# Single-column Newton steps with per-partition scalars, and weight slabs subtracted in four pieces, in a two-block transformer kernel

## The chip, the cores and the metric

The kernel runs on one core of one Trainium2 chip. The metric is the device time of one execution in microseconds (us), as the median of several runs. A core has a matrix engine (PE, with its weight loads as PEld), a vector engine (DVE, VectorE), an activation engine (ACT, ScalarE), a GpSimd engine (POOL) and a queue engine that only starts transfers (SP). Each runs its own instructions in program order and waits on semaphores for the others.

## The reference

The reference is two transformer blocks of two layers each, on 512 tokens of width 1024 in float32. The first block has a gated delta rule layer and a dilated attention layer, the second has two layers with neighbourhood attention, spatial gating and grouped-query attention, modulated by a conditioning vector. A SwiGLU feed-forward net follows each of the four. What matters for the change is that each sublayer begins or ends with a normalisation of every token, and that each holds large products with weight matrices:

```python
def _rmsnorm(x, w):
    xf = x.astype(jnp.float32)
    y = xf * lax.rsqrt(jnp.mean(xf * xf, axis=-1, keepdims=True) + RMS_EPS)
    return (y * w.astype(jnp.float32)).astype(x.dtype)

def layer_norm(x):
    xf = x.astype(jnp.float32)
    mu = jnp.mean(xf, -1, keepdims=True)
    var = jnp.mean(jnp.square(xf - mu), -1, keepdims=True)
    return ((xf - mu) * lax.rsqrt(var + LN_EPS)).astype(x.dtype)

def swiglu(h, w_in, w_out):
    a, b = h @ w_in[:, :D_FF], h @ w_in[:, D_FF:]
    return (jax.nn.silu(a) * b) @ w_out

# second block, layer l
mod = split_cols((sc @ w_mod[l] + b_mod[l])[:, None, :], (D_MODEL,) * N_MOD)
h = modulate(x, sh1, sc1)
y, yc = mixing_sublayer(h, hc, w_in[l], ...)
x = layer_norm(ALPHA * x + g1 * y) * ln1_g[l] + ln1_b[l]
x = layer_norm(ALPHA * x + g2 * swiglu(modulate(x, sh2, sc2), ...)) * ln2_g[l] + ln2_b[l]
```

## The kernel before

Tokens lie on the 128 partitions in blocks of 128 rows: four blocks of the sequence (tile `x`) and two of the context (tile `cx`).

**Products.** Each float32 product is made of three passes in a reduced format: a value is split into a high part (`hi`) and the rest (`lo`), and the matrix engine adds hi·hi, hi·lo and lo·hi. Weights come as slabs of 128 partitions by up to 1024 columns. `Slabs.pump` (line 345) does three things for a slab: it starts the transfer into a buffer `wraw` on SP's queue, copies it rounded into `whi` on ACT (line 365), and subtracts on POOL into `wlo` (line 366, through `Build.sub`, line 444). The buffer `wraw` is free for the next transfer when the subtraction has read it. The pair `whi`, `wlo` goes to `mm_a` or `mm_b` (lines 466 and 482), which run all passes that read `whi` first and those that read `wlo` behind them, and comes back through `done` (line 378). There are two buffers and two pairs in the first layer (`grow`, line 570), one buffer and two pairs more from its end on (line 1077). On the activations' side POOL makes the rests `xl` and `hl`, and `qs` in the attention parts, and some additions into `x`, all in the same queue as the slabs.

**Normalisations.** `rsqrt` (line 447) takes the inverse square root on DVE: two instructions make a first guess, then three Newton steps follow. In `rsqrt`, `f` is the number of columns. Where it is 1 (one value for each token) a step is two `scalar_tensor_tensor` instructions; where it is more, a step is three. It is called with one column by `norm_rms` (line 529), by `ln_scale` (line 1689), `modulate` (line 1698) and `norm_half` (line 1739), and by two norms inside the attention layers; the query and key norms and those of the first layer call it with two to eight columns. In the trace the step's tiles are `rs_t` (the helper `t`), `rs_x` (the value `x`), and `rs` or `four` (the result `out`).

**Order of the work.** `Weave` (line 162) interleaves the streams: it keeps an estimated clock for each engine, adds the estimated cost of each instruction as it is written (line 172; for POOL 100 ns and 2.2 ns a column, for DVE 75 ns and 1.04 ns a column where a tile is narrow), and lets a stream go on when its estimated time has come. The order of every engine's instructions follows from these estimates.

**The modulation vectors** are made beside the feed-forward nets of the first block: DVE multiplies 96 tiles of `w_mod` (tile `mw`) into the sum `macc`, 128 by 1024 each.

All instructions carry the line of one recording helper (line 138), so the rows are told apart by their tiles.

Of the kernel before, what the change touches and what calls it, by code (L numbers as in the profile page):

```python
# [9 lines left out]
F32 = mybir.dt.float32  # L10
# [3 lines left out]
ALU = mybir.AluOpType  # L14
# [107 lines left out]
def _free(ap):  # L122
    n = 1
    for s in ap.shape[1:]:
        n *= s
    return n
# [202 lines left out]
class Slabs:  # L329
# [15 lines left out]
    def pump(self):  # L345
        nc, b = self.b.nc, self.b
        go = True
        while go:
            go = False
            if self.raw and self.loaded < len(self.seq):  # L350
                arr, plan, key, _ = self.seq[self.loaded]
                off, _, nk, _, n = PLANS[plan][0][key]
                raw = self.raw.pop(0)
                src = b.A[arr][off:off + 128 * nk * n].rearrange("(p n) -> p n", p=128)
                nc.sync.dma_start(raw[:, :nk * n], src)
                self.inraw.append(raw)
                self.loaded += 1
                go = True
            if self.pair and self.split < self.loaded:
                arr, plan, key, lo_eng = self.seq[self.split]  # L360
                _, _, nk, _, n = PLANS[plan][0][key]
                e = nk * n
                raw = self.inraw.pop(0)
                hi, lo = pr = self.pair.pop(0)
                nc.scalar.copy(hi[:, :e], raw[:, :e])
                b.sub(lo[:, :e], raw[:, :e], hi[:, :e].bitcast(F32), lo_eng)
                self.raw.append(raw)
                self.ready[self.split] = ((arr, key), pr, nk, e)
                self.split += 1
                go = True  # L370
# [12 lines left out]
class Build:  # L383
# [63 lines left out]
    def rsqrt(self, out, src, scale, eps):  # L447


        v = self.nc.vector  # L450
        shp = list(src.shape)
        f = _free(src)
        x = self.small.tile(shp, F32, name="rs_x", tag=f"rs_x{f}")
        t = self.small.tile(shp, F32, name="rs_t", tag=f"rs_t{f}")
        v.tensor_scalar(x, src, float(scale) * 2.0 ** 26, float(eps) * 2.0 ** 26, ALU.mult, ALU.add)
        v.tensor_scalar(out.bitcast(I32), x.bitcast(I32), -0.5, float(0x5F3759DF - 2 ** 31),
                        ALU.mult, ALU.add)
        for c in (3.0, 12.0, 768.0):
            if f == 1:
                v.scalar_tensor_tensor(t, out, x, out, ALU.mult, ALU.mult)  # L460
            else:
                v.tensor_mul(t, out, out)
                v.tensor_mul(t, t, x)
            v.scalar_tensor_tensor(out, t, -c, out, ALU.add, ALU.mult)

    def mm_a(self, slab, outs, first=True, last=True):
# [1222 lines left out]
    def ln_scale(self, xb, eps=1e-6, st=None):  # L1689

        v = self.nc.vector
        t, rs, nb = self.four((0, 2), (2, 3), (3, 4))
        v.bn_aggr(t, self.stats(xb, st))
        self.rsqrt(rs, t[:, 1:2], 1.0, eps)
        v.scalar_tensor_tensor(nb, t[:, 0:1], -1.0, rs, ALU.mult, ALU.mult)
        return rs, nb

    def modulate(self, l, jj, xb, s, oh, ol, total=None):


        nc = self.nc
        xn = yield from self.xn.take()
        if total is None:
            rs, nb = self.ln_scale(xb)
        else:
            v = nc.vector
            nm, ss, rs, nb = self.four()
            v.tensor_scalar(nm, total, -1.0 / 1024, None, ALU.mult)
            yield
            nc.scalar.activation(xn, xb, AF.Square, bias=nm, accum_out=ss)  # L1710
            yield
            self.rsqrt(rs, ss, 1.0 / 1024, 1e-6)
            v.tensor_mul(nb, nm, rs)
        yield
        nc.scalar.activation(xn, xb, AF.Identity, bias=nb, scale=rs)
        yield
        for h in range(2):
            ps = (yield from self.psS.take()).rearrange("p (k t) -> p k t", k=4)
            for k in range(4):
                c = (4 * h + k) * 128  # L1720
                nc.tensor.transpose(ps[:, k], xn[:, c:c + 128], self.ident)
            yield
            hf = xn[:, 512 * h:512 * h + 512].rearrange("p (k t) -> p k t", k=4)
            for k in range(4):
                kk = 4 * h + k
                sc = self.modc[:, l, jj + 1, s, kk:kk + 1]
                sh = self.modc[:, l, jj, s, kk:kk + 1]
                if k < 3:
                    nc.scalar.activation(hf[:, k], ps[:, k], AF.Identity, bias=sh, scale=sc)
                else:  # L1730
                    nc.vector.tensor_scalar(hf[:, k], ps[:, k], sc, sh, ALU.mult, ALU.add)
            self.psS.rel()
            yield
            nc.scalar.copy(oh(h), hf)
            yield
            nc.gpsimd.tensor_sub(ol(h), hf, oh(h).bitcast(F32))
        self.xn.rel()
# [838 lines left out]
```

## Time and profile before

| what | before |
|---|---|
| median of 3 runs | 3430.48 us (3426.53 to 3433.2) |
| the profiled execution | 3435.41 us, of which the span that the profile shows is 3433.6 us |
| PE busy | 3123.7 us (91%) |
| DVE busy | 1735.3 us (51%), 4221 instructions |
| ACT busy | 1257.0 us (37%) |
| POOL busy | 1440.1 us (42%), 987 instructions |
| granted clock, mean of the span | 0.947 |

Matmuls overlap each other in the pipeline, so the busy time of PE says only when it had work. An engine's idle time is read with what ended it: the engine whose signal came last before the instruction. The busy time of a DVE or POOL instruction is the time from its start to its end, so time in which it has started and cannot go on is in it; one instruction that takes many times the median of its group is read in that way.

### The profile page before, as it was taken

The page shows a single profiled execution, that of the slowest core. Times are in us where ns is not written, and L with a number is a line of the kernel's source. Part 1 is how long each engine was busy: PE and PEld are TensorE (multiplying, and loading weights), DVE is VectorE, ACT ScalarE, POOL GpSimd, SP SyncE. Part 2 cuts the span into 40 slices and gives each one's busy share as a digit, 9 for nine tenths or more (in the row PEclk, how much of TensorE's full clock was granted, in tenths as well). Part 3 has the DMA queues.
Part 4 walks back from the last instruction along what each step waited for, and adds up shares of the span by engine and source line. Part 5 has one row for each costly group of instructions (what it writes and reads, how often), then busy time and mean ns, then how long its engine had stood idle before and what let it go on. Part 6 is the DMA issues. An engine that isn't in the chain of part 4 may idle for free.

```text
span 3433.6 us, 44377 instructions
## 1 busy us (share of the span) xinstructions
PE 3123.7 (91%) x16596; PEld 2696.9 (79%) x16596; DVE 1735.3 (51%) x4221; ACT 1257.0 (37%) x2542; POOL 1440.1 (42%) x987
## 2 busy tenths in 40 slices
PE   7889888999999979999899897999998799869998
PEld 5678767777998767788788777888886789758886
DVE  6975598543464697213644755121015855751113
ACT  4443322222454422333455635212122555543322
POOL 2313344554323245555523325434445534355555
PEclk9989989999999989999999899999999899889999
DMA  3111255432222267323101212111111111242221
GB/s 106 63 33 62 87 178 172 158 122 95 68 63 68 74 210 244 124 94 118 51 24 44 74 41 80 62 65 65 62 67 53 52 39 54 66 122 94 98 98 68
DMA packets 99449, 301.82 MB, mean 88 GB/s; under 512 B 18673, under 2 KB 26017, under 8 KB 99233
## 3 DMA queue, kind: packets, MB, share of 16 engines
q1 hardware_dynamic: 74000, 236.36, 20.3%
q10 hardware_dynamic: 25232, 62.62, 5.7%
q8 instruction: 131, 2.15, 0.3%
q14 instruction: 86, 0.70, 0.1%
HBM read 290.98 MB, written 7.95 MB: 87 GB/s over the span
## 4 chain that ended last, share of the span: by engine, by line
PE 67%; DVE 23%; issue 4%; ACT 3%; DMA 2%; POOL 1%; ACTq 0%; SPq 0%; DVEq 0%; POOLq 0%
PE b L138 37%; PE m L138 24%; PE s L138 6%; DVE macc L138 5%; DVE rs_t L138 4%; DVE x L138 2%; DVE four L138 1%; ACT xn L138 1%; DMA mw<-w_mod 1%; DVE w2k L138 1%; DVE qrs L138 1%; DVE cx L138 1%; DVE tmp L138 1%; DVE T L138 1%; DVE th L138 1%
## 5 line engine op out<-in xcount | busy, mean ns | idle before, releaser
L138 POOL TENSOR_TENSOR wloa<-wrawa,whia 128x1024 fp32r<-128x1024 f32 (+2 forms) x164 | 391.9, 2391 | 617.8 <-ACT whia L138 375.3
L138 DVE SCALAR_TENSOR_TENSOR th<-th,b 128x512 f32<-128x512 f32 x88 | 60.3, 685 | 720.3 <-ACT th L138 720.3
L138 POOL TENSOR_TENSOR wlob<-wrawa,whib 128x1024 fp32r<-128x1024 f32 (+1 forms) x123 | 297.7, 2423 | 301.2 <-ACT whib L138 191.2
L138 ACT CAST whia<-wrawa 128x1024 fp32r<-128x1024 f32 (+2 forms) x164 | 168.3, 1027 | 401.8 <-PE b L138 162.0
L138 PE MATMUL b<-xh,whib 128*128 128x512 f32 (+1 forms) x768 | 288.6, 381 | 24.2 <-DVE th L138 16.8
L138 PE MATMUL b<-xh,whia 128*128 128x512 f32 (+1 forms) x768 | 286.7, 379 | 14.1 <-DVE th L138 12.1
L138 PE MATMUL b<-xl,whia 128*128 128x512 f32 (+1 forms) x768 | 285.2, 377 | 2.0 <-POOL xl L138 2.0
L138 PE MATMUL b<-xl,whib 128*128 128x512 f32 (+1 forms) x768 | 286.7, 379 | 0.0
L138 DVE SCALAR_TENSOR_TENSOR macc<-mw,cv,macc 128x1024 f32<-128x1024 f32 x140 | 247.9, 1812 | 16.1 <-DMA mw<-w_mod 15.6
L138 ACT CAST whib<-wrawa 128x1024 fp32r<-128x1024 f32 (+1 forms) x123 | 125.7, 1022 | 327.8 <-PE b L138 164.5
L138 POOL TENSOR_TENSOR wloa<-wrawb,whia 128x1024 fp32r<-128x1024 f32 (+2 forms) x61 | 141.6, 2321 | 189.5 <-ACT whia L138 120.2
L138 PE MATMUL m<-xh,whia 128*128 128x512 f32 (+2 forms) x520 | 188.3, 367 | 23.6 <-DVE T L138 10.1
L138 POOL TENSOR_TENSOR wlob<-wrawb,whib 128x1024 fp32r<-128x1024 f32 (+1 forms) x61 | 149.8, 2456 | 131.3 <-ACT whib L138 85.4
L138 POOL TENSOR_TENSOR hl<-th,hh 128x512 fp32r<-128x512 f32 (+1 forms) x110 | 151.8, 1389 | 101.4 <-ACT hh L138 97.0
L138 PE MATMUL b<-xh,wlob 128*128 128x512 f32 (+1 forms) x768 | 194.0, 373 | 0.0
L138 PE MATMUL b<-xh,wloa 128*128 128x512 f32 (+1 forms) x768 | 192.2, 372 | 0.0
L138 PE MATMUL m<-xl,whia 128*128 128x512 f32 (+2 forms) x520 | 184.9, 360 | 3.0 <-POOL xl L138 2.9
L138 PEld LDWEIGHTS b<-xh,whib 128*128 128x128 f32 x768 | 148.0, 193 | 47.3 <-issue 11.9
L138 PEld LDWEIGHTS b<-xh,whia 128*128 128x128 f32 x768 | 147.1, 191 | 36.4 <-issue 13.6
L138 PE MATMUL m<-whib,xh 128*128 128x512 f32 (+3 forms) x432 | 162.6, 379 | 13.8 <-ACT xh L138 12.8
L138 PE MATMUL m<-whia,xh 128*128 128x512 f32 (+3 forms) x440 | 170.8, 392 | 4.6 <-ACT xh L138 2.8
L138 PE MATMUL m<-whia,xl 128*128 128x512 f32 (+3 forms) x440 | 167.3, 383 | 0.4 <-DVE xl L138 0.3
(459 smaller groups left out, 8025.7 us busy)
## 6 DMA issues: line engine op xcount, KB each, us to landing
mw<-w_mod ACTq DMA_DIRECT2D x96, 512.0 KB, 4.3
wrawa<-ffn_w_in SPq DMA_DIRECT2D x60, 512.0 KB, 3.3
wrawa<-w_ffn_in SPq DMA_DIRECT2D x56, 512.0 KB, 3.3
wrawa<-gdn_w_in SPq DMA_DIRECT2D x32, 512.0 KB, 3.3
wrawb<-w_ffn_in SPq DMA_DIRECT2D x32, 512.0 KB, 3.3
wrawa<-w_ffn_out SPq DMA_DIRECT2D x32, 512.0 KB, 3.3
wrawb<-ffn_w_in SPq DMA_DIRECT2D x28, 512.0 KB, 3.3
wrawa<-ffn_w_out SPq DMA_DIRECT2D x28, 512.0 KB, 3.3
```

The lines of the kernel that those rows point to most:

```text
L138: r = f(*a, **k)
```

## The change

The Newton step on one column becomes two `tensor_scalar` instructions: each reads one tensor, and the other factors come as values per partition. Two further products of one-column tiles (lines 1695 and 1713) become the same kind of instruction. The subtraction of a weight slab is issued in pieces of 256 columns: four for a slab of 1024, three for 768, two for 512, one for less. Which engine runs what does not change, nor do the buffers. The planner's estimate of POOL's work for a slab grows with the number of pieces.

```diff
@@ Slabs.pump
                 nc.scalar.copy(hi[:, :e], raw[:, :e])
-                b.sub(lo[:, :e], raw[:, :e], hi[:, :e].bitcast(F32), lo_eng)
+                for c in range(0, e, 256):
+                    p = slice(c, min(e, c + 256))
+                    b.sub(lo[:, p], raw[:, p], hi[:, p].bitcast(F32), lo_eng)
                 self.raw.append(raw)
@@ Build.rsqrt
         for c in (3.0, 12.0, 768.0):
             if f == 1:
-                v.scalar_tensor_tensor(t, out, x, out, ALU.mult, ALU.mult)
-            else:
-                v.tensor_mul(t, out, out)
-                v.tensor_mul(t, t, x)
+                v.tensor_scalar(t, out, x, out, ALU.mult, ALU.mult)
+                v.tensor_scalar(out, t, -c, out, ALU.add, ALU.mult)
+                continue
+            v.tensor_mul(t, out, out)
+            v.tensor_mul(t, t, x)
             v.scalar_tensor_tensor(out, t, -c, out, ALU.add, ALU.mult)
@@ Build.ln_scale
-        v.scalar_tensor_tensor(nb, t[:, 0:1], -1.0, rs, ALU.mult, ALU.mult)
+        v.tensor_scalar(nb, t[:, 0:1], -1.0, rs, ALU.mult, ALU.mult)
@@ Build.modulate
-            v.tensor_mul(nb, nm, rs)
+            v.tensor_scalar(nb, nm, rs, None, ALU.mult)
```

## Rows read from the trace of the kernel before

**Rows 1.** The page: busy time by engine, and the chain by engine.

```profile
PE 3123.7 (91%) x16596; PEld 2696.9 (79%) x16596; DVE 1735.3 (51%) x4221; ACT 1257.0 (37%) x2542; POOL 1440.1 (42%) x987
...
PE 67%; DVE 23%; issue 4%; ACT 3%; DMA 2%; POOL 1%; ACTq 0%; SPq 0%; DVEq 0%; POOLq 0%
```

**Rows 2.** Windows: stretch, us, busy of each engine (instructions), clock, DMA.

```profile
415.00:830.00 415.00, 379.35 (x1749) 311.94 (x1750) 260.45 (x248) 105.78 (x130) 205.49 (x90) 0.96 0.45 149
...
2050.00:2110.00 60.00, 41.68 (x250) 37.04 (x249) 49.91 (x145) 32.93 (x60) 26.43 (x18) 0.86 0.21 71
...
3010.00:3065.00 55.00, 23.98 (x130) 20.93 (x131) 39.82 (x107) 25.01 (x45) 25.14 (x15) 0.69 0.48 142
```

**Rows 3.** Waits of PE: who was waited for, total us, times, longest.

```profile
PE s L138 <- ACT xn L138: 54.1, 19, 16.8
PE b L138 <- DVE th L138: 42.7, 12, 7.2
...
PE m L138 <- POOL xl L138: 5.3, 5, 2.9
```

**Rows 4.** Timeline of DVE from 841 us: start, us, instruction.

```profile
842.56 0.16 DVE L138 SCALAR_TENSOR_TENSOR rs<-rs_t,rs 128x1 f32<-128x1 f32 x1
842.76 1.82 DVE L138 SCALAR_TENSOR_TENSOR rs_t<-rs,rs_x 128x1 f32<-128x1 f32 x1
844.61 1.74 DVE L138 SCALAR_TENSOR_TENSOR rs<-rs_t,rs 128x1 f32<-128x1 f32 x1
```

**Rows 5.** Timeline of POOL in the same stretch.

```profile
842.70 1.86 POOL L138 TENSOR_TENSOR wloa<-wrawa,whia 128x768 fp32r<-128x768 f32 x1 [11.88 <-PE s L138]
844.51 1.82 POOL L138 TENSOR_TENSOR wlob<-wrawb,whib 128x768 fp32r<-128x768 f32 x1
```

**Rows 6.** Tile `four`: count, ns min/median/max, first and last start, shape.

```profile
L138 DVE SCALAR_TENSOR_TENSOR rs_t<-four,rs_x x156: 165/217/2445, 1241.5 to 3428.8; 128x1 f32<-128x1 f32 x156
L138 DVE SCALAR_TENSOR_TENSOR four<-rs_t,four x156: 132/159/2271, 1248.4 to 3429.1; 128x1 f32<-128x1 f32 x156
L138 DVE TENSOR_SCALAR rs_x<-four x52: 106/147/158, 1232.3 to 3423.2; 128x1 f32<-128x1 f32 x52
```

**Rows 7.** Tile `rl`, the same columns: one tensor and a scalar per partition.

```profile
L138 DVE TENSOR_SCALAR o<-s,rl x120: 265/282/286, 1711.3 to 2999.8; 128x64 f32<-128x64 f32 x120
```

**Rows 8.** Groups of DVE by shape: count, busy us, mean ns, idle before.

```profile
L138 DVE SCALAR_TENSOR_TENSOR rs_t<-four,rs_x 128x1 f32<-128x1 f32 x156 | 61.6, 415 | 1.5
...
L138 DVE SCALAR_TENSOR_TENSOR rs_t<-rs,rs_x 128x1 f32<-128x1 f32 x138 | 47.7, 350 | 2.3
...
L138 DVE SCALAR_TENSOR_TENSOR four<-rs_t,four 128x1 f32<-128x1 f32 x156 | 42.5, 288 | 1.4
...
L138 DVE SCALAR_TENSOR_TENSOR rs<-rs_t,rs 128x1 f32<-128x1 f32 x138 | 33.0, 242 | 1.7
```

**Rows 9.** Windows of tile `rs_t` alone on DVE: stretch, us, busy (instructions), clock, DMA.

```profile
1190.00:1265.00 75.00, 15.29 (x35) 0.84 0.64 211
...
2050.00:2110.00 60.00, 21.02 (x68) 0.86 0.21 71
...
2600.00:2690.00 90.00, 27.37 (x91) 0.85 0.16 49
...
3010.00:3065.00 55.00, 17.79 (x48) 0.69 0.48 142
```

**Rows 10.** Groups of POOL by shape, columns as in rows 8.

```profile
L138 POOL TENSOR_TENSOR wloa<-wrawa,whia 128x1024 fp32r<-128x1024 f32 x151 | 370.5, 2455 | 569.5 <-ACT whia L138 357.7 <-PE m L138 103.2 <-issue 46.9
...
L138 POOL TENSOR_TENSOR hl<-th,hh 128x256 fp32r<-128x256 f32 x22 | 16.2, 737 | 0.3 <-ACT hh L138 0.3
```

**Rows 11.** Tile `macc`, columns as in rows 6.

```profile
L138 DVE SCALAR_TENSOR_TENSOR macc<-mw,cv,macc x140: 1239/1280/3435, 449.2 to 1388.7; 128x1024 f32<-128x1024 f32 x140
```

**Rows 12.** The page's group of the same instructions: count, busy us, mean ns.

```profile
L138 DVE SCALAR_TENSOR_TENSOR macc<-mw,cv,macc 128x1024 f32<-128x1024 f32 x140 | 247.9, 1812 | 16.1 <-DMA mw<-w_mod 15.6
```

**Rows 13.** Timeline of POOL from 700 us, beside two such instructions.

```profile
710.70 3.38 POOL L138 TENSOR_TENSOR wlob<-wrawa,whib 128x1024 fp32r<-128x1024 f32 x1
```

## The prediction

> **What bounds the kernel now.** I read the page first. The matrix engine is busy for 91% of the span, and the chain that ended last lies on it for 67% and on DVE for 23% [rows 1]. So the gain of a change on DVE and POOL lies in the 310 us in which PE has no work (3433.6 less 3123.7), and in the clock. The windows tell where that is. In a feed-forward stretch PE is busy for 379 of 415 us at a granted clock of 0.96. Between the layers it is busy for 42 of 60 us and for 24 of 55 us, and the clock falls to 0.86 and 0.69, while DVE is busy for 50 and 40 us [rows 2]. There the normalisations of the blocks run one behind the other, and DVE sets the pace. The waits of PE say the same: 54 us for `xn`, the normalised rows, and 43 us for `th`, the gate of the feed-forward net, which DVE makes in the same queue as the `macc` sums; for POOL's rests `xl` it is 5 us [rows 3]. Nothing in these rows waits for a weight slab.
>
> The third view is the timeline. Two Newton instructions on one column take 1.82 and 1.74 us, where the one before them took 0.16 [rows 4]. POOL started a slab at 842.70 and ended it at 844.56, and the DVE instruction that started at 842.76 ended at 844.58; the next slab began at 844.51 and ended at 846.33, the next DVE instruction at 846.35 [rows 4, 5]. So a DVE instruction with two tensors in SBUF that starts while POOL runs a subtraction ends just behind it, and the two engines take turns, one instruction each. The tile view shows how common that is: the step's instructions have medians of 217 and 159 ns and maxima over 2.2 us, the length of a slab, while a `tensor_scalar` on the same columns, with one tensor, has a median of 147 and never took over 158 ns in 52 times [rows 6]. A scalar per partition does not bring the wait back: `o<-s,rl`, one tensor from PSUM and such a scalar from SBUF, stays between 265 and 286 ns in 120 times [rows 7].
>
> **The change part by part.**
>
> *Waits of the one-column steps.* The four groups hold 156 + 138 = 294 steps and 61.6 + 47.7 + 42.5 + 33.0 = 184.8 us [rows 8]. By the medians a step without waits takes 217 + 159 = 376 ns [rows 6], so 294 take 110.5 us, and 74 us are waits for POOL. The change takes away the second tensor, and I take these 74 us as gone from the instructions. Not all of it is on the path. In four stretches between layers I take each row of tile `rs_t` less 188 ns (half a step) for each instruction: 15.29 - 6.6 = 8.7, 21.02 - 12.8 = 8.2, 27.37 - 17.1 = 10.3, of which I take 8 since some of its 91 instructions are norms of several columns, and 17.79 - 9.0 = 8.8 [rows 9]. That makes 34 us where DVE sets the pace. The other 40 us lie in the attention layers, where PE has other work, and at a few shorter norms. The POOL instruction that held the step up is still there, and the next DVE instruction with two tensors can meet its end. I count three quarters of the 34 and half of the 40: 25.5 + 20 = 45.5 us.
>
> *Price of the new instructions.* No row has a `tensor_scalar` on one column with scalars per partition. The nearest are 147 ns without one, and the pair 217 and 159 ns, in which one scalar from a tile costs 58 ns more than a constant [rows 6]. The first new instruction has two such scalars: between 205 ns (147 + 58) and 263 ns (147 + 116). The second has one: 205 ns. The lower end is a step of 410, the upper one of 468 ns; I take the upper, since a scalar more is one read more. That is 92 ns more than the 376 of a step without waits: 10 us for the 108 or so steps of the four stretches, and for the other 186 steps, counted by half as above, 8.6 us. Both lie on the path where the gain lies. Net of the first edit: 45.5 - 18.6 = 27 us. The two further products (lines 1695 and 1713) gain and lose by the same rule, a few microseconds at most; I put them at nothing.
>
> *Pieces, price on POOL.* A slab of 1024 takes 2455 ns on the mean, a subtraction of 256 columns 737 ns [rows 10]. Four pieces take between 2455 (if all of the fixed part overlaps) and 2948 ns. Two POOL instructions overlap a little: 842.70 + 1.86 is 844.56 and the next began at 844.51 [rows 5], so I take 4 × 737 - 3 × 50 = 2.8 us, or 0.35 us more for a slab. Queued behind the pieces on POOL are the rests `xl`, `hl` and `qs` and the additions into `x`; on SP's queue the next transfer waits for the last piece. POOL is busy for 205 of 415 us in the feed-forward stretch [rows 2], so the cover is its idle half; where it is gone, between layers, PE waits for `xl` five times [rows 3]. I put the loss at 4 us; its bounds are 0 and 0.35 us for each of some 400 slabs, 140 us, if nothing hid it.
>
> *Pieces, gain on DVE.* A DVE instruction that still has two tensors waits for the rest of a piece, at most 0.74 us, in place of the rest of a slab, at most 2.4. The `macc` sums are the largest such group: 140 take 247.9 us, 1812 ns on the mean, with a median of 1280 [rows 11, 12], so 69 us are waits. Scaled by 737 to 2455 they fall to 21 us. The 48 us come free on DVE in the feed-forward stretches, where PE waits 43 us for `th` [rows 3]; I count a quarter of 48, 12 us. For steps of several columns and the like, chains of dependent instructions, taking turns with four pieces costs about what one slab did; where several slabs stand in POOL's queue a step gets four turns in a slab's time. I count 4 us for these; the bounds are a loss of 10 and a gain of 20.
>
> *The planner* counts 4 × (100 + 2.2 × 256) = 2653 for a slab in place of 2353, so it sends streams with POOL work out a little later. Nothing in the trace prices that; by the smallness of the shift I take 0, with ±10 us.
>
> **The sum.** 27 - 4 + 12 + 4 = 39 us less. The profiled execution took 3435.4 us (span 3433.6), 5 us over the median of the runs. Against the median it is 3430.5 - 39 = 3391 us.
>
> **The rivals.**
>
> *The waits move on.* POOL's work is unchanged, and the large DVE instructions in between (adds and norms of 512 and 1024 columns) have two tensors too. If they meet the slab's end in place of the small ones, a quarter of the 34 and an eighth of the 40 us is left, 13.5, less 18.6 for the new instructions; with 12 from `macc` and the other terms gains are 7 us: 3423. For it speaks that in the serial stretches DVE has little else to do than such work; against it that the pieces shorten what can be met.
>
> *Everything pays.* All 74 us less 27, half of PE's waits for `th`, and the clock: between layers it is granted at 0.69 to 0.86 [rows 2], and shorter gaps give some of it back. 47 + 21 + some 18 is 86: 3344.
>
> *The new instructions wait too.* Then only the prices stay: 18.6 us more, 16 us less by the pieces, 4 us more on POOL: 3437. The 52 instructions with a maximum of 158 ns speak against it [rows 6]. The Trainium skill names the rule by which it would come: by "SBUF — State Buffer", section "Who interferes with whom", `tensor_scalar` can enter a mode with two ports, and then contends with GpSimd. [...]
>
> *Slower: POOL falls behind.* A slab beside two `macc` sums takes 3.38 us in place of 2.4, for one turn lost [rows 13]. Four pieces can lose four turns. If each of the 140 sums holds a piece up by 1.0 us, POOL gets 140 us more to do, beside 0.35 us a slab. It decides from the point where POOL no longer has idle time in the stretch: 205 us and some 70 in 415 is short of that [rows 2], so it needs a burst. If half of the 140 came to PE as late slabs or late `hl`, it would be 70 more: 3391 + 70 = 3461.
>
> **How the numbers follow.** The forecast, 3391, has 0.58, with its own range of 3360 to 3418; the moved waits 0.17, half of it within 0.2%; everything pays 0.12; new instructions that wait 0.04; POOL behind 0.09. About 0.2% (7 us) is what a measurement of this kernel tells from no change. Faster by more than that: 0.58 + 0.08 + 0.12, less a little for the forecast's edge, 0.77. Within it: 0.12. Slower: 0.11. The range reaches into the best case at 3345 and ends at 3432; POOL behind and half of the best case are left out.
>
> **What would show it.** Right: the one-column steps have maxima under 300 ns and about 468 ns a step; `macc` has a mean near 1430 and maxima near 2.0 us; POOL has some 1100 instructions more and about 130 us more busy time; PE's waits for `xn` and `th` fall, and the clock of the stretches between layers rises. Wrong: DVE instructions of 512 and 1024 columns take up the waits, with means well over 1.3 us between layers; or PE's waits for `xl` or for slabs grow; or new one-column instructions with maxima at the length of a piece. The prediction fails on size if the four stretches shrink by much less or more than the 25 us counted there.

## The result, and the profile after

The changed kernel takes 3337.4 us, the median of 4 runs (3334.5 to 3338.9), beside 3431.4 us for the kernel before in the same session (4 runs, 3426.5 to 3433.2). The ratio is 0.9727, with an interval of 0.971 to 0.9744: 94 us less where 39 were forecast, and below the low end of the range. The profiled execution has a span of 3337.1 us.

The page of the changed kernel, busy time by engine (us, share of the span, instructions), which answers to [rows 1]:

```profile
PE 3100.8 (93%) x16596; PEld 2679.4 (80%) x16596; DVE 1626.4 (49%) x4221; ACT 1254.2 (38%) x2542; POOL 1716.3 (51%) x2163
```

DVE has 109 us less to do with the same 4221 instructions. POOL has 276 us more, in 1176 instructions more. Span less busy time gives the time in which PE stands: 309.9 us before, 236.3 after. So 73.6 of the 96.5 us of span come from there. The other 22.9 us are PE's own work: the same 16596 products took less time. I come back to that below.

The steps on one column, tile `four` in the changed kernel (count, ns min/median/max), which answer to [rows 6]:

```profile
L138 DVE TENSOR_SCALAR rs_t<-four,rs_x x156: 254/267/276, 1170.6 to 3331.5; 128x1 f32<-128x1 f32 x156
L138 DVE TENSOR_SCALAR four<-rs_t,four x156: 166/208/216, 1174.7 to 3331.8; 128x1 f32<-128x1 f32 x156
```

No instruction is held up any more: the maxima are 276 and 216 ns where they were 2445 and 2271. A step takes 267 + 208 = 475 ns. DVE's groups of the changed kernel (busy us, mean ns), which answer to [rows 8]:

```profile
L138 DVE TENSOR_SCALAR rs_t<-four,rs_x 128x1 f32<-128x1 f32 x156 | 38.7, 267 | 1.8
L138 DVE TENSOR_SCALAR rs_t<-rs,rs_x 128x1 f32<-128x1 f32 x138 | 36.3, 268 | 2.0
...
L138 DVE TENSOR_SCALAR four<-rs_t,four 128x1 f32<-128x1 f32 x156 | 29.3, 207 | 1.8
L138 DVE TENSOR_SCALAR rs<-rs_t,rs 128x1 f32<-128x1 f32 x138 | 27.8, 208 | 1.6
```

They sum to 132.1 us, where the four groups of [rows 8] held 184.8.

The `macc` sums, first the group and then the tile's row (ns min/median/max), which answer to [rows 12] and [rows 11]:

```profile
L138 DVE SCALAR_TENSOR_TENSOR macc<-mw,cv,macc 128x1024 f32<-128x1024 f32 x140 | 226.2, 1654 | 15.6 <-DMA mw<-w_mod 15.1
```

```profile
L138 DVE SCALAR_TENSOR_TENSOR macc<-mw,cv,macc x140: 1228/1752/2533, 424.9 to 1306.9; 128x1024 f32<-128x1024 f32 x140
```

The mean and the maximum fell (1812 to 1654, 3435 to 2533), but the median rose, from 1280 to 1752. Before, most sums met no slab and a few lost a whole turn. Now most lose about half a microsecond to a piece.

POOL's largest group of the changed kernel, which answers to [rows 10]:

```profile
L138 POOL TENSOR_TENSOR wloa<-wrawa,whia 128x256 fp32r<-128x256 f32 x638 | 503.8, 821 | 518.2 <-ACT whia L138 488.6 <-PE m L138 26.0 <-issue 3.0
```

PE's waits in the changed kernel (us in total, times, longest), which answer to [rows 3]:

```profile
PE s L138 <- ACT xn L138: 28.9, 9, 10.8
PE b L138 <- DVE th L138: 18.5, 7, 3.9
...
PE m L138 <- POOL xl L138: 14.3, 6, 8.0
```

To see where the gain lies I cut both traces at the same products, counted from the start. The next rows are windows of three stretches: the first layer, its feed-forward net, and the second layer's attention (us, then busy time and instructions of PE, PEld, DVE, ACT, POOL, then the granted clock and the transfers). First the kernel before:

```profile
76.50:418.00 341.50, 303.86 (x1835) 256.41 (x1834) 241.59 (x632) 134.26 (x357) 100.09 (x51) 0.91 0.17 57
...
418.00:830.10 412.10, 376.75 (x1744) 310.19 (x1743) 258.98 (x246) 104.23 (x128) 204.90 (x89) 0.96 0.45 149
...
852.10:1194.00 341.90, 323.55 (x1733) 300.16 (x1733) 186.53 (x657) 150.23 (x371) 97.85 (x47) 0.95 0.21 67
```

And the changed kernel:

```profile
73.70:397.50 323.80, 295.60 (x1835) 250.87 (x1834) 229.00 (x632) 133.80 (x356) 114.89 (x147) 0.93 0.18 59
397.50:785.40 387.90, 370.39 (x1744) 306.10 (x1743) 238.12 (x246) 103.87 (x128) 289.14 (x288) 0.99 0.49 159
801.30:1128.40 327.10, 316.62 (x1732) 293.88 (x1731) 177.73 (x660) 150.39 (x372) 117.39 (x162) 0.98 0.24 74
```

These three stretches give 17.7, 24.2 and 14.8 us, over half of the whole. In each, DVE does the same instructions in less time (12.6, 20.9 and 8.8 us), PE stands that much less (9.4, 17.8 and 7.9 us), and its own busy time falls too (8.3, 6.4 and 6.9 us) while the mean granted clock rises. Of the forecast's 39 us, 15.5 (25.5 - 10) were to come from four stretches between the layers, 11.4 from the attention layers and shorter norms, 12 from `macc` in the feed-forward nets and 4 from the chains of small instructions, less 4 for POOL.

### The profile page after: what moved, and what is told of

Same layout as the page of the kernel before. It is cut to its first block, busy times and chain, and to the rows that moved or that the text cites. A ratio compares the mean times of both kernels' runs of the same rounds, so it can differ in the third digit from the quotient of the medians.

```text
span 3337.1 us, 46608 instructions
## 1 busy us (share of the span) xinstructions
PE 3100.8 (93%) x16596; PEld 2679.4 (80%) x16596; DVE 1626.4 (49%) x4221; ACT 1254.2 (38%) x2542; POOL 1716.3 (51%) x2163
## 4 chain that ended last, share of the span: by engine, by line
PE 50%; DVE 8%; ACT 2%; DMA 2%; POOL 2%; issue 1%; SPq 0%; DVEq 0%; ACTq 0%; POOLq 0%
PE b L138 31%; PE m L138 16%; PE s L138 4%; DVE macc L138 2%; DVE rs_t L138 1%; DMA mw<-w_mod 1%; DVE w2k L138 1%; ACT xn L138 1%; DVE x L138 1%; DVE qrs L138 1%; ACT w2k L138 0%; POOL xl L138 0%; POOL wloa L138 0%; POOL wlob L138 0%; DMA gr<-grow 0%
## 5 line engine op out<-in xcount | busy, mean ns | idle before, releaser
L138 POOL TENSOR_TENSOR wloa<-wrawa,whia 128x256 fp32r<-128x256 f32 x639 | 504.3, 820 | 530.2 <-ACT whia L138 488.6
L138 POOL TENSOR_TENSOR wlob<-wrawa,whib 128x256 fp32r<-128x256 f32 x475 | 374.6, 821 | 217.1 <-ACT whib L138 192.3
L138 POOL TENSOR_TENSOR wloa<-wrawb,whia 128x256 fp32r<-128x256 f32 x232 | 183.3, 821 | 140.9 <-ACT whia L138 138.5
L138 POOL TENSOR_TENSOR wlob<-wrawb,whib 128x256 fp32r<-128x256 f32 x239 | 198.3, 861 | 89.5 <-ACT whib L138 88.9
L138 DVE SCALAR_TENSOR_TENSOR macc<-mw,cv,macc 128x1024 f32<-128x1024 f32 x140 | 226.2, 1654 | 15.6 <-DMA mw<-w_mod 15.1
L138 PE MATMUL m<-xh,whia 128*128 128x512 f32 (+2 forms) x520 | 183.6, 358 | 13.4 <-ACT xh L138 4.2
L138 PE MATMUL m<-whib,xl 128*128 128x512 f32 (+3 forms) x432 | 162.4, 378 | 6.3 <-POOL xl L138 6.3
```

What stands on the lines that cost most here:

```text
L138: r = f(*a, **k)
```

## The experiments

All have three rounds of timing beside runs of the kernel before, whose medians were 3426.9 us beside the first four kernels, 3428.4 beside the next four and 3428.8 beside the last three. My theory after the result: both edits do what the prediction says, but every instruction of DVE with two tensors in SBUF that meets a subtraction of POOL pays for the rest of it, and nearly all of that time is on the path, in the chains of small instructions too. The rivals: the planner's new order makes the gain; the pieces gain through `macc` alone; the gain of the new instructions is not their freedom from waits.

### Each edit by itself

The first kernel has the new one-column instructions and whole slabs. The part in `rsqrt` is shown; the two products at lines 1695 and 1713 are changed as well.

```diff
             if f == 1:
-                v.scalar_tensor_tensor(t, out, x, out, ALU.mult, ALU.mult)
...
+                v.tensor_scalar(t, out, x, out, ALU.mult, ALU.mult)
+                v.tensor_scalar(out, t, -c, out, ALU.add, ALU.mult)
+                continue
...
```

> The new one-column instructions alone; a slab is subtracted in one instruction as before. Theory A (the sum of the prediction): these instructions bring 27 us, so about 3403 us. Theory B (the pieces carry the result): the one-column waits of 90 us vanish from the rows, but the next two-tensor instruction meets the end of the slab, so 10 us or less, about 3420 us. Theory C (the two edits need each other): as B here, and less than 60 us for the pieces alone.

The second has the pieces and the old steps.

```diff
-                b.sub(lo[:, :e], raw[:, :e], hi[:, :e].bitcast(F32), lo_eng)
+                for c in range(0, e, 256):
+                    p = slice(c, min(e, c + 256))
+                    b.sub(lo[:, p], raw[:, p], hi[:, p].bitcast(F32), lo_eng)
```

> The pieces alone; the one-column steps are those of the kernel before. Theory A: 12 us, about 3419 us. Theory B: 70 us or more, about 3355 us, with the first layer some 15 us and the first feed-forward net some 20 us shorter, as in the changed kernel. Theory C: about 3380 us, with one-column instructions that now wait for a piece, up to 0.7 us each.

The steps alone took 3390.9 us, 0.9898 (0.9879 to 0.9917): 36 us less. The pieces alone took 3356.3, 0.9797 (0.9782 to 0.9813): 71 us less. So the steps brought more than any of the three theories had for them, and the pieces what theory B had. Together they would be 107; both edits at once gave 94, so about 13 us were to be had by either. The pages' busy rows, the steps alone and then the pieces alone:

```profile
PE 3114.6 (92%) x16596; PEld 2686.5 (79%) x16596; DVE 1703.3 (50%) x4221; ACT 1256.8 (37%) x2542; POOL 1449.9 (43%) x987
```

```profile
PE 3106.2 (92%) x16596; PEld 2683.0 (80%) x16596; DVE 1669.5 (50%) x4221; ACT 1256.1 (37%) x2542; POOL 1693.0 (50%) x2163
```

With spans of 3392.7 and 3358.9 us PE stands 278.1 and 252.7 us, 32 and 57 less than before, while DVE's work falls by 32 and 66. So a microsecond of waiting taken from DVE is worth about one on PE, in the steps and in the pieces alike. Stretch by stretch, cut at the same products (us against before):

| stretch (us in the kernel before) | steps | pieces | both |
|---|---|---|---|
| first layer (77 to 418) | -1.8 | -18.2 | -17.7 |
| its feed-forward net (418 to 830) | -1.3 | -20.1 | -24.2 |
| second layer's attention (852 to 1194) | -0.6 | -14.0 | -14.8 |
| its feed-forward net (1265 to 1601) | -1.0 | +0.9 | -8.7 |
| mixing layers of the second block (1601 to 2051, 2695 to 3011) | -13.4 | -9.1 | -6.0 |
| between the layers (830, 1194, 2051, 2600, 3011) | -19.7 | -13.3 | -22.5 |
| the rest | -3.1 | -1.0 | -2.6 |

Each column is one profiled execution. How far a row can be trusted, a kernel of the next section shows: it does the same instructions as the kernel before in another order, takes within 0.2% of its time, and yet differs from it by -3.5, -2.4 and -3.7 us in the first three rows and by 4.7 in the fourth. Single rows of under some 5 us are not read here.

The two edits work in different places. The steps gain between the layers and in the mixing layers, the pieces above all in the first block. The second layer's feed-forward net has its 8.7 us only with both edits. That is not explained; the pieces with the planner's old count have -4.6 in that row where the pieces here have +0.9, so half of it can lie in the order alone. In the first block's two attention layers no `macc` sum runs (the first starts at 449.2 us, [rows 11], and none lies in the second of them), so 32 of the pieces' 75 us of span can't come through `macc`.

### The planner's count

One kernel keeps one subtraction and lets the planner count four pieces, the other makes four pieces and lets it count one.

```diff
-                b.sub(lo[:, :e], raw[:, :e], hi[:, :e].bitcast(F32), lo_eng)
+                b.tc.nc.gpsimd.tensor_sub(lo[:, :e], raw[:, :e], hi[:, :e].bitcast(F32))
+                for c in range(0, e, 256):
+                    p = slice(c, min(e, c + 256))
+                    b.w.note("POOL", "tensor_sub", (lo[:, p], raw[:, p]), {})
```

> The kernel before in all its instructions, but the planner counts each slab as pieces (2653 in place of 2353), so only the order of the instructions may change. Theory D (the new order brings the gain): 30 us or more less than before in the first layer and the first feed-forward net. Theories A and B: within 10 us of the kernel before, 3425 to 3441 us.

```diff
-                b.sub(lo[:, :e], raw[:, :e], hi[:, :e].bitcast(F32), lo_eng)
+                for c in range(0, e, 256):
+                    p = slice(c, min(e, c + 256))
+                    b.tc.nc.gpsimd.tensor_sub(lo[:, p], raw[:, p], hi[:, p].bitcast(F32))
+                b.w.note("POOL", "tensor_sub", (lo[:, :e], raw[:, :e]), {})
```

> The pieces alone, with the planner counting a slab as one subtraction as before. Theory B: as with the pieces counted, within 10 us of that run. Theory D: close to the kernel before, above 3415 us.

The count alone took 3432.3 us, 1.0014 (1.0002 to 1.0025), and the pieces with the old count 3360.9, 0.9806 (0.9789 to 0.9823), the same as with the new one. Stretch by stretch, too, the pieces with the old count give what they gave with the new one: -19.9, -19.1 and -13.8 us in the first three rows of the table above. The planner is not the cause.

### The size of a piece

Pieces of 512 and of 128 columns, in place of 256, with the old steps.

```diff
-                for c in range(0, e, 256):
+                for c in range(0, e, 512):
...
```

> The steps of the kernel before; each slab is subtracted in pieces of 512 columns (two for a slab). Theory B1 (what counts is how long one DVE instruction can be held up): the longest hold falls from 2.4 to 1.3 us, so about half of the 70 us of the pieces of 256, 3385 to 3400 us. Theory B2 (any break is enough, since DVE then gets its turn): as with pieces of 256, 3350 to 3370 us.

```diff
-                for c in range(0, e, 256):
+                for c in range(0, e, 128):
...
```

> The steps of the kernel before; pieces of 128 columns, eight for a slab, 0.46 us each. Theory B1: the longest hold falls to 0.46 us, 10 to 20 us less than with pieces of 256, 3335 to 3350 us, unless the longer slab (8 x 0.46 less overlap, 3.3 us in place of 2.4) makes POOL late. Theory E (POOL's own time takes over): slower than with pieces of 256, 3360 us or more, with PE waiting for POOL's rests or for slabs.

Pieces of 512 took 3387.1 us, 0.9884 (0.9863 to 0.9905), pieces of 128 took 3369.2, 0.9833 (0.981 to 0.9856). So 1024, 512, 256 and 128 columns give 0, 41, 71 and 59 us: theory B1 holds for 512 columns, theory E for 128. To see why, I counted in each trace the DVE instructions that took over 0.1 us more than the lower quartile of the same group in the kernel before; I call them held:

| columns in a piece | held instructions | us held, in sum | us for one | POOL busy us |
|---|---|---|---|---|
| 1024 | 266 | 332 | 1.25 | 1440.1 |
| 512 | 375 | 299 | 0.80 | 1542.4 |
| 256 | 511 | 265 | 0.52 | 1693.0 |
| 128 | 561 | 216 | 0.39 | 1930.8 |

Shorter pieces hold more instructions, but not in proportion: from 1024 to 256 twice as many are held, each for two fifths of the time. POOL pays for it in the last column, 253 us for four pieces and 491 for eight. Up to four its idle time covers that. At eight it no longer does everywhere, as PE's waits show, first with pieces of 256 and then of 128:

```profile
PE m L138 <- POOL xl L138: 3.7, 5, 1.6
...
PE b L138 <- POOL xl L138: 2.5, 4, 0.8
```

```profile
PE b L138 <- POOL xl L138: 14.1, 6, 8.9
...
PE m L138 <- POOL xl L138: 9.9, 7, 5.5
```

The rests `xl` wait behind the longer work on POOL, 24 us in place of 6. The last feed-forward net, with little for DVE to gain (57 us of work in 350), shows the loss alone. This is its window with pieces of 256, then of 128 (with nine products more):

```profile
2990.00:3334.70 344.70, 344.70 (x1579) 288.01 (x1579) 57.17 (x87) 104.58 (x107) 228.11 (x282) 1.00 0.26 91
```

```profile
2996.00:3349.70 353.70, 347.68 (x1588) 290.42 (x1588) 57.28 (x87) 108.85 (x117) 266.62 (x533) 1.00 0.28 96
```

### One kind of slab only

Pieces of 256 for the slabs of the first layer's input weights alone.

```diff
-                b.sub(lo[:, :e], raw[:, :e], hi[:, :e].bitcast(F32), lo_eng)
+                for c in range(0, e, 256 if arr == "gdn_w_in" else e):
+                    p = slice(c, min(e, c + (256 if arr == "gdn_w_in" else e)))
+                    b.sub(lo[:, p], raw[:, p], hi[:, p].bitcast(F32), lo_eng)
```

> The steps of the kernel before; pieces of 256 only for the slabs of the first layer's input product (33 of 409). Theory B: the first layer is shorter by some 18 us, as with pieces everywhere, and no later stage changes, about 3410 us. Rival F (the new order of the whole program carries the gain): other stages change as well, by 10 us or more, or the first layer keeps its length.

It took 3414.2 us, 0.9963 (0.9947 to 0.9979): 14 us less. The windows of the first layer and of the feed-forward net behind it:

```profile
74.80:398.90 324.10, 294.27 (x1835) 250.59 (x1834) 230.19 (x632) 133.85 (x356) 110.95 (x122) 0.94 0.17 59
398.90:812.10 413.20, 380.36 (x1743) 313.29 (x1742) 258.42 (x246) 104.39 (x129) 207.11 (x89) 0.96 0.44 149
```

The first layer has the whole gain of the pieces (324.1 us, where all slabs in pieces gave 323.3 and whole slabs 341.5), the net behind it none (413.2 against 412.1). So the gain belongs to the stretch in which the slabs are subtracted, and the first layer's comes without any `macc` sum. Behind it the second layer's feed-forward net was 4.0 us longer and the first mixing layer 2.4. That is no more than the order alone makes (4.7 us in the first of them), and the profiled execution, 3422.8 us, was 8.6 over the median of its ten.

### No reading by POOL

POOL writes zeros into most of the low half instead of subtracting, for about the same time (twice 0.9 us for 960 columns and twice 0.3 us for the 32 that are still subtracted).

```diff
-                b.sub(lo[:, :e], raw[:, :e], hi[:, :e].bitcast(F32), lo_eng)
+                g = b.tc.nc.gpsimd
+                g.tensor_sub(lo[:, :32], raw[:, :32], hi[:, :32].bitcast(F32))
+                g.memset(lo[:, 64:e].bitcast(F32), 0.0)
+                g.memset(lo[:, 64:e].bitcast(F32), 0.0)
+                g.tensor_sub(lo[:, 32:64], raw[:, 32:64], hi[:, 32:64].bitcast(F32))
+                b.w.note("POOL", "tensor_sub", (lo[:, :e], raw[:, :e]), {})
```

> The steps of the kernel before; in place of the subtraction of a slab POOL subtracts 32 columns, fills the rest of the tile twice with zeros and subtracts 32 columns at the end, about 2.4 us as before, so the low parts of the weights are left out. A fill reads no SBUF. Theory B (the gain is the removal of waits at the shared read of SBUF): DVE instructions with two tensors no longer wait for slabs, and the time falls by more than the pieces brought, to 3290 to 3340 us. Rival F (the gain of the pieces comes from POOL's order or from earlier slabs, not from waits of DVE): within 20 us of the kernel before.

It took 3251.1 us, 0.9486 (0.9462 to 0.9509): 177 us less, and 39 below the range that was expected. With the new instructions as well:

> The new one-column instructions together with GpSimd writing zeros to most of each low half instead of subtracting, so that its work on slabs reads nearly nothing (the low parts of the weights beyond the first 64 columns are left out of the product). The same fill with the old instructions took 3251 us, and its one-column steps still waited 37 us in sum. Theory (the new instructions gain by not waiting and are longer otherwise): with the slabs' reading gone, of the 37 us about half lies on the path, against some 10 to 19 us for the longer instructions, so 3245 to 3260 us; the edit that was worth 36 us beside whole slabs is worth under 10 here. Rival (the new instructions gain by something else, as fewer operands or the planner's order): again some 30 to 40 us, 3211 to 3221 us.

That took 3244.9 us, 0.9462 (0.9444 to 0.948), at the low end of the theory's range. The busy row of the page of the first of the two, and its one-column steps (old instructions):

```profile
PE 3069.7 (94%) x16596; PEld 2660.9 (82%) x16596; DVE 1501.3 (46%) x4221; ACT 1258.7 (39%) x2542; POOL 1384.1 (43%) x2214
```

```profile
L138 DVE SCALAR_TENSOR_TENSOR rs_t<-four,rs_x x156: 166/215/1602, 1117.4 to 3244.1; 128x1 f32<-128x1 f32 x156
```

POOL is as busy as before (1384 us against 1440), and yet DVE needs 234 us less and PE stands 130 us less. So DVE waits not because POOL works, but because of what POOL's instruction does: a fill, which reads no tensor, lets most of DVE's instructions run. It is not that the fills come in shorter instructions: those of 960 columns take 0.90 us each, where the pieces of 256 take 0.81 to 0.85 on the mean, and pieces leave 265 us of held time and bring 71 us where fills leave 97 and bring 177. Beside that fill the new instructions are worth 6 us in place of 36, and their intervals overlap: the rival by which they gain something else is out. Of the 184 us of span that the first of the two saves (3433.6 less 3249.5) 130 are time in which PE no longer stands, and 54 are PE's own work. PE here multiplies zeros in most of the low halves, and whether that bears on its granted clock no run tests. So it is not shown that all of this can be had with the subtraction kept; the pieces and the steps have brought 94 us.

### Small pieces where they helped

Both edits, and pieces of 128 in the first layer, where they had given 29.8 us in place of 18.2.

```diff
-                for c in range(0, e, 256):
-                    p = slice(c, min(e, c + 256))
+                w = 128 if arr == "gdn_w_in" else 256
+                for c in range(0, e, w):
+                    p = slice(c, min(e, c + w))
```

> Both edits of the change, but the slabs of the first layer's input weights (gdn_w_in) in pieces of 128 columns instead of 256. With pieces of 128 everywhere the first layer's stage had shortened by 29.8 us against 18.2 us with 256, and the stages behind it had lost part of their gain. Theory (what a piece costs is what the instruction of VectorE behind it still waits, so the best size is a matter of the stage: many short dependent instructions and an idle GpSimd want small pieces): about 11 us under the changed kernel, 3320 to 3330 us, all of it in the first layer. Rival (the order of the whole program shifted in that run, and the 29.8 us belonged to that order): 3333 to 3345 us, no different from the changed kernel.

It took 3332.3 us, 0.9721 (0.9705 to 0.9736), no different from the changed kernel's 0.9727. Yet the first layer did shorten, from 323.8 to 315.9 us. In the profiled execution nearly as much was lost in the first mixing layer. The windows of the two stretches in this kernel, and of the mixing layer in the changed one:

```profile
1509.30:1967.30 458.00, 415.57 (x2446) 373.16 (x2445) 266.20 (x956) 231.40 (x609) 178.64 (x313) 0.91 0.17 55
...
72.30:388.20 315.90, 291.65 (x1835) 247.58 (x1834) 223.09 (x629) 133.14 (x353) 128.19 (x243) 0.95 0.19 61
```

```profile
1518.50:1969.20 450.70, 407.62 (x2446) 364.87 (x2445) 265.70 (x956) 230.80 (x609) 178.70 (x313) 0.93 0.18 56
```

DVE, ACT and POOL do the same work in the same time, and PE stands 42.4 us against 43.1. But the same 2446 products took 8.0 us more, at a mean granted clock of 0.91 in place of 0.93. How much of that belongs to this kernel is not shown. The profiled execution is the slowest of its four, 3336.4 us at a mean granted clock of 0.957; the other three took 3327.9 to 3332.9 us at 0.960 and 0.961, where the changed kernel's four took 3334.5 to 3338.9 at 0.959 and 0.960. So the mechanism holds in its place, and the median came out 2 us over the theory's range and just under the rival's: the runs do not tell whether the total kept some of the 8 us or none.

### The other subtractions of POOL

Both edits, and the subtractions for `xl` and for half of the `hl` of 512 columns in two pieces. The part for `xl` is shown.

```diff
-            nc.gpsimd.tensor_sub(ol(h), hf, oh(h).bitcast(F32))
+            o1, h1 = ol(h), oh(h)
+            for p in (slice(0, 2), slice(2, 4)):
+                nc.gpsimd.tensor_sub(o1[:, p], hf[:, p], h1[:, p].bitcast(F32))
...
```

> Both edits of the change, and in addition the subtractions of 512 columns on GpSimd that split the activations (88 of hl, 44 of xl, some 1.3 to 1.5 us each in the changed kernel) in two pieces of 256. Theory (any long subtraction of GpSimd holds VectorE, slab or not): halving some 130 of them saves at most a quarter of a microsecond or so for each instruction of VectorE caught, 5 to 15 us, less some 0.2 us of GpSimd for each split, of which only the xl are waited for by the tensor engine (17 us in sum): 3322 to 3340 us. Rival (these splits lie on the path themselves, xl before the next products, so what the pieces add is paid at once): 3340 to 3352 us.

It took 3337.4 us, 0.9737 (0.9721 to 0.9754), the same as the changed kernel. The groups show the splits (44 of the 88 `hl`, with another layout, stayed whole, so fewer were split than the expectation says):

```profile
L138 POOL TENSOR_TENSOR hl<-th,hh 128x256 fp32r<-128x256 f32 x110 | 89.5, 838 | 37.4 <-ACT hh L138 37.4
L138 POOL TENSOR_TENSOR hl<-th,hh 128x512 fp32r<-128x512 f32 x44 | 75.1, 1706 | 39.0 <-ACT hh L138 39.0
L138 POOL TENSOR_TENSOR xl<-xn,xh 128x256 fp32r<-128x256 f32 x88 | 66.7, 788 | 60.8 <-ACT xh L138 60.7
```

The second layer's attention became another 6 us shorter and the first layer's feed-forward net 3, and the second block took as much back: 3 us in the first mixing layer and 6 around the end of the third feed-forward net. The time is outside the rival's range and inside the theory's, but the theory's range held the changed kernel's own 3337.4, so the run speaks for neither.

## Why the prediction was wrong

**The first edit was right, a little small.** The waits go, the step costs 475 ns where 468 were worked out, and the four stretches between the layers became 13.5 us shorter in the run with the steps alone (1.2, 2.2, 3.7 and 6.4), against 25.5 - 10 = 15.5 counted. The other half was too small: 11.4 us counted, 27 measured in the span. Half of the waits in the attention layers and in the shorter norms was taken to hide beside PE's work; in the mixing layers (13.4 us) and at 830 us (6.2 us) it did not. The edit gave 36 us for 27.

**The step that failed is the pieces' gain on DVE,** 12 + 4 us for what measured 71 net. It has three parts.

*Chains of dependent instructions* were said to pay for four pieces about what they paid for a slab, 4 us with bounds of -10 and +20. The attention layers of the first block, whose held instructions are nearly all in such chains, gave 18.2 and 14.0 us. The timeline shows why the argument fails. This is DVE in the first layer, before (start, us, instruction), and POOL beside it:

```profile
248.42 2.23 DVE L138 TENSOR_TENSOR tmp<-Pk,T 128x49 f32<-128x49 f32 x1
250.57 0.74 DVE L138 SCALAR_TENSOR_TENSOR cx<-m,cw,cx 128x511 f32<-128x511 f32 x1
251.23 0.19 DVE L138 TENSOR_TENSOR T<-T,tmp 128x49 f32<-128x49 f32 x1
```

```profile
248.24 2.35 POOL L138 TENSOR_TENSOR wloa<-wrawa,whia 128x1024 fp32r<-128x1024 f32 x1 [3.01 <-ACT whia L138]
```

And the same chain a few instructions on, in the changed kernel, beside four pieces:

```profile
236.77 0.20 DVE L138 TENSOR_TENSOR tmp<-Pk,T 128x35 f32<-128x35 f32 x1
236.89 0.74 DVE L138 SCALAR_TENSOR_TENSOR cx<-m,cw,cx 128x510 f32<-128x510 f32 x1
237.55 0.19 DVE L138 TENSOR_TENSOR T<-T,tmp 128x35 f32<-128x35 f32 x1
237.67 0.75 DVE L138 SCALAR_TENSOR_TENSOR cx<-m,cw,cx 128x509 f32<-128x509 f32 x1
238.34 0.72 DVE L138 TENSOR_TENSOR tmp<-Pk,T 128x28 f32<-128x28 f32 x1
```

```profile
236.18 2.84 POOL L138 TENSOR_TENSOR wloa<-wrawa,whia 128x256 fp32r<-128x256 f32 x4 [1.59 <-ACT whia L138]
```

Before, one instruction of 0.19 us stood until the slab ended, and everything behind it stood too. The four pieces end at steps of 0.71 us, at about 236.9, 237.6, 238.3 and 239.0. Two of the chain's instructions (at 236.77 and 237.55) ran at such an end and lost nothing. Between them DVE ran `cx`, one of whose tensors lies in PSUM and which is not held (0.74 us beside a piece and without one). Only one was held, for 0.53 us. A chain takes a turn with a piece only if its next two-tensor instruction is ready while that piece runs; the prediction gave it all four. The count over the whole first layer: 30 held instructions with 45.4 us before, 65 with 33.9 us with the pieces alone.

*`macc`* was to fall to a mean of 1430 ns; it fell to 1654. These are long instructions with two tensors each, back to back, and here the turns are real, so the median rose. 140 × (1812 - 1654) ns are 22 us freed, not 48. But of that nearly all was worth its time, not a quarter: in the first feed-forward net PE stood 17.5 us in place of 35.3. Two errors that nearly cancel: 12 counted, about 18 found.

*The clock* stood in a rival alone. In the run with the pieces PE's own work is 17.5 us shorter, in that with the steps 9.1, in the changed kernel 22.9, with the same 16596 products. The mean granted clock went from 0.91 to 0.93 in the first layer and from 0.96 to 0.99 in its feed-forward net. As a mean of the two levels, 2.4 and 1.2 GHz, that is some 8% of the net's time at the lower level before (33 us) and 2% after (8 us). PE stood half as long in that net when it did so. Less idle time and a higher clock go together in all three stretches; no run separates them. In the first layer part of it can be the order alone: with only the planner's count changed PE stands 1.1 us longer there, and its own work is still 4.4 us shorter than before, at 0.93:

```profile
77.20:415.40 338.20, 299.49 (x1834) 252.97 (x1833) 242.06 (x632) 134.18 (x356) 99.94 (x51) 0.93 0.17 57
```

In the feed-forward net that kernel has the 0.96 of the kernel before, and every kernel with pieces of 256 in that net has 0.97 to 0.99. As far as the link holds, a stall costs twice: for its own length, and for the products behind it that run at 1.2 GHz.

**The price of the pieces on POOL** was too low in itself: 0.35 us a slab counted, 0.68 measured. The groups of the slabs sum to 981 us before and 1260 after, since a piece has a mean of some 820 ns and not 737: pieces wait for DVE as DVE waits for them. What PE pays for it was too high, 4 us: with the pieces alone PE waits for `xl` 6 us, as before. The 14.3 us of the changed kernel come with the first edit. This is the same row with the steps alone:

```profile
PE m L138 <- POOL xl L138: 13.1, 8, 5.4
```

**The planner,** 0 with ±10, was right: +0.14% for its count alone.

**The rivals.** The time is nearest to the case in which everything pays (3344). Its halves on `th` (24 us of 42.7 gone) and on the clock (18 counted, 22.9 found) hold. Its 47 us for the steps do not, and it has no term for the chains, so it comes near by another sum. The waits did not move on to the large instructions, and POOL did not fall behind with four pieces. With eight it began to. The new instructions don't wait; that this holds for `tensor_scalar` on one column and not on several is shown below. The pieces do lose time to DVE, as that rival said, but among PE's waits in the changed kernel there is none for a `wlo`.

## What to carry to other kernels

Where two engines shut each other out for the length of one instruction, the long instruction sets the price, and it pays to cut it as far as the fixed part and the idle time of its engine allow; the best size is found by trying two or three. A gain of that kind is counted by the sum of the held time over all instructions, small ones in chains among them, and on the engine that paces a stretch it counted here at nearly its full length, with what the clock gave back on top. Changing the held instruction to a kind that is not held works too, but the kind has to be looked up in the trace with its number of columns: with its tensors in SBUF, `tensor_scalar` was free on one column alone. And a count of turns holds only where the next instruction of the held kind is ready at once.

## What the runs showed of the hardware

Whether two instructions shut each other out hangs on both. I took the DVE instructions with all their tensors in SBUF that started while one of POOL's ran and had more than 0.15 us left beyond their own undisturbed length, in groups of at least four, and counted the held ones by the rule above. The left column has POOL's instructions on two tensors, nearly all subtractions and additions, in the kernel before; the right one has the fills of zeros in the kernel with fills and old steps:

| DVE instruction | beside two tensors on POOL | beside a fill |
|---|---|---|
| two tensors | 180 of 186 held | 0 of 151 held |
| `tensor_scalar`, 2 to 1024 columns | 24 of 24 held | 19 of 19 held |
| `tensor_scalar`, 1 column | 0 of 35 held | 0 of 14 held |

In the changed kernel, with the new steps among them, it is 0 of 204 for `tensor_scalar` on one column. So the prediction's reason for the new instructions, that they have only one tensor, is not enough, and neither is the theory's class of two tensors: on several columns an instruction with one tensor waits as well, and even for a fill, which reads nothing. An instance on 8 columns, in the kernel with fills, first POOL and then DVE:

```profile
97.70 0.90 POOL L369 MEMSET wloa<- 128x960 f32 x1
```

```profile
97.82 0.80 DVE L138 TENSOR_SCALAR rs_x<-sc 128x8 f32<-128x8 f32 x1 [0.77 <-ACT junk L138]
98.66 0.17 DVE L138 TENSOR_SCALAR sc<-rs_x 128x8 int32<-128x8 int32 x1
```

The first took 0.80 us, where the median of its eight is 0.17, and ended 0.02 us behind the fill. The first instruction of each `macc` sum is of this kind, on 1024 columns. Its row (ns min/median/max) in the kernel before, and then with fills:

```profile
L138 DVE TENSOR_SCALAR macc<-mw,cv x20: 742/748/2892, 447.9 to 1369.9; 128x1024 f32<-128x1024 f32 x20
```

```profile
L138 DVE TENSOR_SCALAR macc<-mw,cv x20: 733/750/1596, 401.6 to 1229.8; 128x1024 f32<-128x1024 f32 x20
```

In sum, 252 of the 332 us of held time in the kernel before end with a slab's subtraction. With fills 97 us of held time are left; 19 of them end with a fill, nearly all in `tensor_scalar`, and the rest with POOL's other work, `xl` first.

Executions of one kernel differ, and the granted clock with them. The profiled execution of the kernel with smaller pieces in the first layer took 8.0 us more than the changed kernel for the same 2446 products of the first mixing layer, at 0.91 in place of 0.93, with the other engines' work the same. In that layer the granted clock is below 1 in and behind stretches in which PE stands: in the changed kernel 0.73 in 25 us with 21.6 busy and 0.86 in the next, in the kernel with the smaller pieces 0.76 and then 0.70. Windows of 25 us, the changed kernel and then the other:

```profile
1793.50:1818.50 25.00, 21.56 (x93) 18.20 (x93) 18.41 (x96) 16.52 (x55) 8.45 (x17) 0.73 0.07 22
1818.50:1843.50 25.00, 20.35 (x116) 17.84 (x114) 15.99 (x78) 19.99 (x56) 16.94 (x30) 0.86 0.23 64
```

```profile
1789.10:1814.60 25.50, 22.58 (x108) 19.98 (x109) 18.31 (x92) 17.64 (x60) 9.35 (x20) 0.76 0.01 3
1814.60:1840.00 25.40, 21.43 (x101) 19.67 (x101) 15.13 (x72) 18.22 (x48) 18.58 (x32) 0.70 0.24 78
```

Why the lower level lasted longer there with nearly the same idle time is open; no run here settles it, and the other three executions of that kernel, all faster, have a higher mean clock. So single microseconds won in one place should be judged by the total, with several runs.
